# Lending another operand slot to plain products, and spreading row factors by two-part products, in a convolution and retention trunk

## The chip, the cores and the metric

The kernel runs on one core of one Trainium2 chip. The metric is device time in microseconds of one execution. A core has a matrix engine (TensorE, shown as PE, with its weight loads as PEld), three elementwise engines (VectorE as DVE, ScalarE as ACT, GpSimd as POOL) and SyncE (SP), from which this kernel issues its DMAs. Each engine works off its own queue strictly in the order in which the program was written out.

## The reference, cut to what matters

Sixteen meta rows are put ahead of 2048 rows of width 1024. Everything is float32.

```
hn   = rms_norm(h, norm1_g)
proj = hn @ w_in                            # 1024 x 4096, split into 8 parts
cx, cb, cc, cg, q, k, v, rg = split(proj, 8)
conv_out = cb * conv3(cc * cx) * silu(cg)
q, k = rotary(q, pos) * d**-0.5, rotary(k, pos)
ret  = group_norm(chunked_retention(q, k, v))   # 4 heads of 128, chunks of 128
out  = h + concat(conv_out, ret * silu(rg)) @ w_out
return rms_norm(out, final_g)[:, 16:]
```

The norm of a row is a factor per row, so the kernel multiplies the projected values by it instead of the inputs.

## The kernel before

The 2048 rows are handled as two blocks (r = 0 and 1) of 1024 rows, each as two halves (j) of 512. Per block there are four retention heads (`head`) and then four convolution groups (`conv_group`); each asks for two "quads", products of a 2 x 2 block matrix of weights (each block 4 tiles of 128 x 128 over the depth) with a 2 x 2 block matrix of rows. After both blocks follow eight output quads (`output`) with w_out as the moving side.

A quad is done in one of two ways. `quad` (line 208) forms seven products instead of eight: product number i multiplies a combination of weight blocks `w[i]` with a combination of row blocks `m[i]`. `quad_plain` (line 258) forms the eight plain products from the blocks `m[0]`, `m[7]`, `m[1]`, `m[5]` as they are. The first two quads of block 0, the first of block 1 and the first output quad are plain, since the combinations aren't ready by then. The combinations of the row side are called T1 (`m[3]`), T2 (`m[2]`), T3 (`m[4]`) and T4 (`m[6]`). `block_sums` makes them in the order T1, T2, T4, T3. For block 0 they are made on the spot; for block 1 and for w_out they are made earlier by `prepare`, put in DRAM (`sums_x`, `sums_w`) and fetched by `prepared(m, src, ns)`, where n = 0, 1, 2, 3 stands for T1, T2, T3, T4 (`SUMS`).

Each float32 operand is split into two float32r parts: hi, a rounding on ACT (line 99, or 102 with a scale), and lo, the rest on DVE (line 111, or 103). One product tile is three matmuls, lo by hi, hi by lo and hi by hi; a product of `quad` is 4 x 3 = 12 matmuls of 128 x 512, a plain quad is 96.

The parts of `m[i]` live in slots: one pair of tiles per i and depth tile kt, each a single buffer (`operand`). `m[7]` shares the slot of `m[4]` (`B12 = 4`). The weights of a plain quad also live in such slots: those of the first plain quad in slot 2 (`FIRST_W`), those of the others in slot 3 (`PLAIN_W`), the slot of T1. A slot can be rewritten once the last matmul that reads it is done. The raw weight tiles `ra` have 8 buffers.

The row factors: `row_factors` squares the rows on ACT (line 317), `spread_factors` makes the column of factors `rc`, and `spread` turns that column into a row that stands on all partitions (`rr`). It does so by a diagonal tile on DVE (line 281) and a float32 matmul with ones (line 288). The diagonal takes the tag `rot`, of which there is one buffer; `rotary` uses the same buffer for its products (lines 512 to 514 and the addition at line 108).

`spread` is called five times: for the meta rows (16 factors) and for j = 0, 1 of each block (512 factors).

The order of the work on each queue isn't written by hand: a planner runs the program through its own model of the costs ahead of time and, whenever an engine is free there, gives it the ready instruction that stands first in the program.

In block 0 the steps around the change, in the order of the program, are: splits of the row blocks, weights of both plain quads, `block_sums` with splits of T2 and T4, row factors, head 0 (plain quad, plain quad, `rest` with the splits of T1 and T3, attention), head 1 and so on.

Of the kernel before, what the change touches and what calls it, by code (L numbers as in the profile page):

```python
# [8 lines left out]
F32 = mybir.dt.float32  # L9
F32R = mybir.dt.float32r  # L10
BF16 = mybir.dt.bfloat16
AF = mybir.ActivationFunctionType
ALU = mybir.AluOpType

P = 128
# [6 lines left out]
HB = 512  # L22
NR = 2
BLK = SEQ // NR
CH = HB // P
KH = KT // 2
# [3 lines left out]
HIGH = 400  # L30
BRIEF = 2
BLOCK = ((0, 7), (1, 5))
FIRST_W, PLAIN_W, B12 = 2, 3, 4
SUMS = (3, 2, 4, 6)


# [32 lines left out]
def hybrid_trunk(ctx: ExitStack, tc: tile.TileContext, t, out: bass.AP, chunk_decay):  # L69
# [5 lines left out]
    nc = tc.nc  # L75
    x = t["x"]

    const = ctx.enter_context(tc.tile_pool(name="const", bufs=1))
    small = ctx.enter_context(tc.tile_pool(name="small", bufs=2))
    sb = ctx.enter_context(tc.tile_pool(name="sb", bufs=2))  # L80
# [15 lines left out]
    def split(hi, lo, src, scale=None, eng=nc.vector):  # L96

        if scale is None:
            nc.scalar.copy(out=hi, in_=src)  # L99
            sub(eng, lo, src, hi.bitcast(F32))  # L100
            return
        nc.scalar.mul(hi, src, scale)
        nc.vector.scalar_tensor_tensor(
            out=lo, in0=src, scalar=scale, in1=hi.bitcast(F32), op0=ALU.mult, op1=ALU.subtract
        )
# [39 lines left out]
    def parts(m, i, kt, src, factor=None):  # L145
        hi, lo = operand(i, kt)
        split(hi, lo, src, factor)
        m[i].append((hi, lo))
# [42 lines left out]
    def prepared(m, src, ns):  # L191

        for n in ns:
            for kt in range(KH):
                a = gen("t")[:, :HB]
                nc.sync.dma_start(a, src[n, kt])
                parts(m, SUMS[n], kt, a)
# [79 lines left out]
    def spread(col, n, dst, squares=None):  # L277

        a = col.shape[1]
        diag = sb.tile([P, HB], F32, name="rot", tag="rot", bufs=1).rearrange("p (a c) -> p a c", a=CH)  # L280
        nc.vector.tensor_tensor(
            out=diag[:n, :a, :n],
            in0=ident[:n, :n].rearrange("p (a c) -> p a c", a=1).broadcast_to([n, a, n]),
            in1=col.rearrange("p (a c) -> p a c", c=1).broadcast_to([n, a, n]),
            op=ALU.mult,
        )
        rp = ps_misc()
        nc.tensor.matmul(
            rp[:, : a * n].rearrange("p (a c) -> p a c", a=a), ones[:n].broadcast_to([n, P]), diag[:n, :a, :n], start=True, stop=True
        )  # L290
        nc.scalar.copy(out=dst, in_=rp[:, : a * n])
        if squares is not None:
            nc.scalar.activation(squares, rp[:, : a * n], AF.Square)

    gain = const.tile([P, KT], F32, name="gain")
    ident = const.tile([P, P], F32, name="ident")
    ones = const.tile([P, 1], F32, name="ones")
    neg_half = const.tile([P, CH], F32, name="neg_half")
    meta_s = const.tile([P, KT, NMETA], F32, name="meta_s")
# [344 lines left out]
    def output(pair, m, final_g):  # L644
        d = mixed[pair // 2]
        loads = [
            lambda a, i=i, k=k: nc.sync.dma_start(a.rearrange("p (k c) -> p k c", k=KH), d[pair % 2, i, k])
            for i in range(2)
            for k in range(2)
        ]  # L650
        ys = [[None, None], [None, None]]
        ss = small.tile([P, 2, 2], F32, name="so", tag="so")
        for i in range(2):
            for j in range(2):
                y = gen("yo")[:, :HB]
                row = (2 * pair + i) * P
                nc.sync.dma_start(y, x[row : row + P, j * HB : (j + 1) * HB])
                ys[i][j] = y
        last = [None]

        def take(i, j, pp, c):
            y = ys[i][j]
            if c is not None:
                add(nc.gpsimd, y, y, c)
            last[0] = nc.vector.tensor_tensor(out=y, in0=pp, in1=y, op=ALU.add)  # L665
            junk = sb.tile([P, HB], F32, name="rot", tag="rot", bufs=1)
            nc.scalar.activation(junk, y, AF.Square, accum_out=ss[:, i, j : j + 1])
            if i == j:
                ys[i][j] = gen("z")[:, :HB]
                nc.gpsimd.tensor_tensor(out=ys[i][j], in0=y, in1=final_g[:, j * HB : (j + 1) * HB], op=ALU.mult)  # L670

        if pair == 0:
            w = plain_parts(loads)
            prepared(m, sums_w, (1, 3))
            quad_plain(w, m, take)
            prepared(m, sums_w, (0, 2))
        else:
            quad(stationary(load_raw(loads)), m, take)
        for i in range(2):
            tot = small.tile([P, 1], F32, name="tot", tag="tot")  # L680
            add(nc.vector, tot, ss[:, i, 0:1], ss[:, i, 1:2])
            rs = small.tile([P, 1], F32, name="rf", tag="rf")
            rsqrt_mean(rs, tot)
            row = (2 * pair + i) * P
            for j in range(2):
                cs = slice(j * HB, (j + 1) * HB)
                y = ys[i][j]
                if i == j:
                    nc.scalar.mul(y, y, rs)
                else:  # L690
                    with tc.issue_after(last[0].ins):
                        nc.vector.scalar_tensor_tensor(
                            out=y, in0=y, scalar=rs, in1=final_g[:, cs], op0=ALU.mult, op1=ALU.mult
                        )
                nc.sync.dma_start(out[row : row + P, cs], y)

    make_identity(nc, ident)
    nc.gpsimd.memset(ones, 1.0)
    nc.gpsimd.memset(neg_half, -0.5)
    warm = const.tile([P, P], BF16, name="warm")  # L700
# [22 lines left out]
    for r in range(NR):  # L723
        f = factors[r]
        rot_t = sb.tile([P, 2, BLK], F32, name="rot_t", tag="rot_t", bufs=1)
        p0 = NMETA + r * BLK

        def load_tables():
            nc.sync.dma_start(rot_t, t["rot"][:, :, p0 : p0 + BLK])

        if r == 0:
            w = [None] * 4
            loads = w_loads(0)

            def begin(half):
                for n in (half, 2 + half):
                    w[n] = plain_part(n, loads[n], FIRST_W)

            m, b = moving(
                load_x(r), gain_of, {(0, 0): lambda: begin(0), (0, KH - 1): lambda: begin(1), (0, KT - 1): normalise_meta}  # L740
            )
            first = [[p for a, p in w]]
            blocks = None, meta_products([a for a, p in w])
            first.append(plain_parts(w_loads(1)))
            load_tables()
            nc.sync.dma_start(cols, t["cols"])
            t3 = [a[:, i * HB : (i + 1) * HB] for a in (row_tile("t3") for _ in range(2)) for i in range(2)]
            t1 = [brief("t1") if n < BRIEF else sb.tile([P, HB], F32, name="t1", tag="tc", bufs=COPIES) for n in range(KH)]
            for kt in range(KH):
                b11, b21, b12, b22 = (b[n * KH + kt] for n in range(4))  # L750
                block_sums(b11, b12, b22, b21, t1[kt], t3[kt], gain_of(kt), gain_of(KH + kt), nc.gpsimd)
                parts(m, 2, kt, b22)
                parts(m, 6, kt, b21)
            for _ in row_factors(0, f):
                pass
            nc.sync.dma_start(causal, t["causal"])
            nc.sync.dma_start(conv_w, t["conv_w"])
            nc.sync.dma_start(ret_g, t["ret_norm_g"])

            def rest():  # L760
                for i, held in ((3, t1), (4, t3)):
                    for kt in range(KH):
                        parts(m, i, kt, held[kt])

            between = (lambda: None, rest)
            later = prepare(load_x(1), sums_x, gain_of)
        else:
            m, b = moving(load_x(r), gain_of)
            first = [plain_parts(w_loads(0))]
            load_tables()  # L770
            prepared(m, sums_x, (1, 3))
            between = (lambda: prepared(m, sums_x, (0, 2)),)
            blocks = None, None
            later = prepare(load_w_out, sums_w)
        for h in range(NG):
            blocks = head(h, r, m, rot_t, f, blocks, lambda: ahead(r, h + 1), *((first, between) if h == 0 else ()))
            if h > 0:
                next(later, None)
                next(later, None)
        steps = row_factors(r + 1, factors[r + 1]) if r < NR - 1 else iter(())  # L780
        for g in range(NG):
            blocks = conv_group(g, r, m, f, blocks, lambda: ahead(r, NG + g + 1))
            for _ in range(3):
                next(steps, None)
# [44 lines left out]
```

## Time and profile before

| What | Value |
|---|---|
| Median of three runs | 902.29 us (902.17 to 903.6) |
| The profiled execution | 903.85 us, its span 902.1 us, 1.75 us around it |
| Mean granted TensorE clock | 0.994 |
| PE busy | 885.0 us (98%), 4407 matmuls |
| DVE busy | 714.6 us (79%) |
| ACT busy | 406.1 us (45%) |
| POOL busy | 398.9 us (44%) |
| Instructions | 12862 |

Matmuls are pipelined, so the busy time of PE overlaps itself: two matmuls of 128 x 512 start some 0.23 us apart while each lasts 0.39 us. Stalls are therefore read from the distance of starts, and from the waits. The profiled execution took 1.56 us more than the median.

### The profile page before, as it was taken

The page shows a single profiled execution, that of the slowest core. Times are in us where ns is not written, and L with a number is a line of the kernel's source. Part 1 is how long each engine was busy: PE and PEld are TensorE (multiplying, and loading weights), DVE is VectorE, ACT ScalarE, POOL GpSimd, SP SyncE. Part 2 cuts the span into 40 slices and gives each one's busy share as a digit, 9 for nine tenths or more (in the row PEclk, how much of TensorE's full clock was granted, in tenths as well). Part 3 has the DMA queues.
Part 4 walks back from the last instruction along what each step waited for, and adds up shares of the span by engine and source line. Part 5 has one row for each costly group of instructions (what it writes and reads, how often), then busy time and mean ns, then how long its engine had stood idle before and what let it go on. Part 6 is the DMA issues. An engine that isn't in the chain of part 4 may idle for free.

```text
span 902.1 us, 12862 instructions
## 1 busy us (share of the span) xinstructions
PE 885.0 (98%) x4407; PEld 727.8 (81%) x4407; DVE 714.6 (79%) x1173; ACT 406.1 (45%) x815; POOL 398.9 (44%) x294
## 2 busy tenths in 40 slices
PE   8998999999999999999999999999999999999996
PEld 5787888888878777788888888888888878788885
DVE  6798888897686776899889899777667697866764
ACT  8771342424344443655333332433333465554553
POOL 0533132323355554461333323345546445777763
PEclk9998999999999999999999999999999999999999
DMA  9711352623234232744125262113231685555532
GB/s 333 239 40 38 104 195 59 205 82 107 79 103 127 78 108 78 253 180 141 38 73 203 73 236 68 50 56 90 57 88 48 210 280 178 162 186 152 182 111 93
DMA packets 76242, 116.94 MB, mean 130 GB/s; under 512 B 7632, under 2 KB 24336, under 8 KB 76176
## 3 DMA queue, kind: packets, MB, share of 16 engines
q1 hardware_dynamic: 76176, 116.11, 40.1%
q8 instruction: 35, 0.57, 0.3%
q14 instruction: 31, 0.25, 0.1%
HBM read 90.92 MB, written 25.17 MB: 129 GB/s over the span
## 4 chain that ended last, share of the span: by engine, by line
PE 83%; DVE 9%; DMA 3%; ACT 2%; issue 2%; POOL 1%; SPq 0%; POOLq 0%; DVEq 0%; ACTq 0%
PE pj L208 66%; PE pj L258 7%; DVE ml L111 2%; DVE wl L111 2%; PE ms L611 2%; PE ms L612 1%; PE ms L601 1%; PE ms L588 1%; PE ms L392 1%; DVE rot L513 1%; DMA ra<-in_w_in 1%; PE ms L635 1%; PE ms L573 1%; DVE rot L512 1%; PE ms L578 1%
## 5 line engine op out<-in xcount | busy, mean ns | idle before, releaser
L208 PE MATMUL pj<-mh,wl 128*128 128x512 f32 x1008 | 400.0, 397 | 1.0 <-ACT tc L215 0.8
L208 PE MATMUL pj<-ml,wh 128*128 128x512 f32 x1008 | 394.2, 391 | 1.1 <-DVE ml L111 1.1
L208 PE MATMUL pj<-mh,wh 128*128 128x512 f32 x1008 | 393.4, 390 | 0.0
L99 ACT CAST wh<-ra 128x512 fp32r<-128x512 f32 x216 | 133.8, 620 | 315.1 <-PE pj L208 272.4
L208 PEld LDWEIGHTS pj<-mh,wl 128*128 128x128 f32 x1008 | 189.6, 188 | 43.1 <-ACT tc L215 2.2
L208 PEld LDWEIGHTS pj<-ml,wh 128*128 128x128 f32 x1008 | 189.8, 188 | 39.6 <-DVE ml L111 1.9
L208 PEld LDWEIGHTS pj<-mh,wh 128*128 128x128 f32 x1008 | 189.6, 188 | 39.8
L111 DVE TENSOR_TENSOR wl<-ra,wh 128x512 fp32r<-128x512 f32 x216 | 192.4, 892 | 36.2 <-ACT wh L99 35.2
L111 POOL TENSOR_TENSOR ra<-ra 128x512 f32<-128x512 f32 x72 | 113.0, 1570 | 82.0 <-DVE qg L556 32.3
L108 POOL TENSOR_TENSOR sa<-ra 128x512 f32<-128x512 f32 x36 | 54.9, 1525 | 122.6 <-DVE wl L111 62.1
L111 POOL TENSOR_TENSOR ra<-sa,ra 128x512 f32<-128x512 f32 x36 | 52.2, 1450 | 98.3 <-DVE wl L111 98.0
L215 ACT COPY tc<-pj 128x512 f32<-128x512 f32 x108 | 62.6, 580 | 0.0
L258 PE MATMUL pj<-ml,mh 128*128 128x512 f32 x128 | 50.8, 396 | 0.1
L258 PE MATMUL pj<-mh,mh 128*128 128x512 f32 x128 | 50.2, 395 | 0.0
L258 PE MATMUL pj<-mh,ml 128*128 128x512 f32 x128 | 48.5, 396 | 1.5 <-DVE ml L111 1.5
L624 POOL TENSOR_TENSOR rp<-rs,neg_half 128x4 f32<-128x4 f32 x16 | 19.9, 1245 | 51.0 <-DVE rs L108 50.8
L466 POOL TENSOR_TENSOR c<-c,rr 128x512 f32<-128x512 f32 x16 | 30.0, 1874 | 24.0 <-DVE c L454 13.6
L108 DVE TENSOR_TENSOR tc<-pj,tc 128x512 f32<-128x512 f32 x32 | 22.0, 688 | 23.4 <-PE pj L208 23.4
L111 DVE TENSOR_TENSOR ml<-t,mh 128x512 fp32r<-128x512 f32 x40 | 36.6, 961 | 0.8 <-ACT mh L99 0.8
L99 ACT CAST wh<-sa 128x512 fp32r<-128x512 f32 x36 | 22.3, 620 | 32.7 <-PE pj L208 32.7
L665 DVE TENSOR_TENSOR yo<-pj,yo 128x512 f32<-128x512 f32 x32 | 22.0, 688 | 18.8 <-POOL yo L108 8.9
L466 POOL TENSOR_TENSOR c<-c,tc 128x512 f32<-128x512 f32 x16 | 27.3, 1706 | 19.0 <-ACT tc L492 17.6
(128 smaller groups left out, 1134.3 us busy)
## 6 DMA issues: line engine op xcount, KB each, us to landing
ra<-in_w_in SPq DMA_DIRECT2D x128, 256.0 KB, 2.7
x<-in_xT SPq DMA_DIRECT2D x48, 256.0 KB, 5.1
w<-in_w_out SPq DMA_DIRECT2D x32, 256.0 KB, 5.0
ra<-mixed SPq DMA_DIRECT2D x32, 256.0 KB, 2.7
yo<-in_x SPq DMA_DIRECT2D x32, 256.0 KB, 4.4
ra<-in_x SPq DMA_DIRECT2D x16, 256.0 KB, 3.7
mixed<-qg SPq DMA_DIRECT2D x16, 256.0 KB, 2.3
sums_x<-x SPq DMA_DIRECT2D x16, 256.0 KB, 2.4
```

Source lines behind the costliest of these rows:

```text
L99: nc.scalar.copy(out=hi, in_=src)
L108: eng.tensor_tensor(out=out, in0=a, in1=b, op=ALU.add)
L111: eng.tensor_tensor(out=out, in0=a, in1=b, op=ALU.subtract)
L208: nc.tensor.matmul(bank, a[:, ks], b, start=first and kt == 0 and n == 0, stop=kt == KH - 1 and n == 2, skip_group_check=not first,)
L215: nc.scalar.copy(out=c, in_=bank)
L258: nc.tensor.matmul(banks[i], a[:, ks], b, start=half + kt + n == 0, stop=half == 1 and kt == KH - 1 and n == 2,)
L392: nc.tensor.matmul(four[i], meta_s[:, i % 2 * KH + kt, :], blocks[i][:, kt * P : (kt + 1) * P], start=kt == 0, stop=kt == KH - 1,)
L466: eng.tensor_tensor(out=out, in0=a, in1=b, op=ALU.mult)
L512: nc.vector.tensor_tensor(out=rot[:h, :w], in0=a[h:], in1=table[h:, 1, :], op=ALU.mult)
L611: nc.tensor.matmul(o[:, cs], pm[:, cs], vt[j][:, cs], start=True, stop=False)
L624: nc.gpsimd.tensor_tensor(out=rp, in0=rs, in1=neg_half.rearrange("p (c a) -> p c a", a=1), op=ALU.pow)
L665: last[0] = nc.vector.tensor_tensor(out=y, in0=pp, in1=y, op=ALU.add)
```

## The change

Three things change. Plain quads after the first put their weights in slot 6, T4's, instead of slot 3, T1's. Accordingly T1 is split where T4 was (together with T2), and T4 where T1 was (together with T3, and after it); the same exchange is made in the two places that fetch from DRAM. And `spread` no longer makes a diagonal: it splits the column of factors into hi and lo, and for each of up to four columns multiplies each part, broadcast over 128 columns as the stationary side, with a float32r unit matrix `ident_r`, so that two matmuls of 128 x 128 add up to the factors of 128 rows. `ident_r` is one more constant, copied once by ACT.

```diff
-FIRST_W, PLAIN_W, B12 = 2, 3, 4
+FIRST_W, PLAIN_W, B12 = 2, 6, 4
...
     def spread(col, n, dst, squares=None):
         a = col.shape[1]
-        diag = sb.tile([P, HB], F32, name="rot", tag="rot", bufs=1).rearrange("p (a c) -> p a c", a=CH)
-        nc.vector.tensor_tensor(
-            out=diag[:n, :a, :n],
-            in0=ident[:n, :n].rearrange("p (a c) -> p a c", a=1).broadcast_to([n, a, n]),
-            in1=col.rearrange("p (a c) -> p a c", c=1).broadcast_to([n, a, n]),
-            op=ALU.mult,
-        )
+        hi, lo = (small.tile([P, CH], F32R, name="ch", tag="ch", bufs=4) for _ in range(2))
+        split(hi[:n, :a], lo[:n, :a], col)
         rp = ps_misc()
-        nc.tensor.matmul(
-            rp[:, : a * n].rearrange("p (a c) -> p a c", a=a), ones[:n].broadcast_to([n, P]), diag[:n, :a, :n], start=True, stop=True
-        )
+        for c in range(a):
+            for p, part in enumerate((hi, lo)):
+                nc.tensor.matmul(
+                    rp[:, c * n : (c + 1) * n], part[:n, c : c + 1].broadcast_to([n, P]), ident_r[:n, :n],
+                    start=p == 0, stop=p == 1,
+                )
...
         if pair == 0:
             w = plain_parts(loads)
-            prepared(m, sums_w, (1, 3))
+            prepared(m, sums_w, (1, 0))
             quad_plain(w, m, take)
-            prepared(m, sums_w, (0, 2))
+            prepared(m, sums_w, (2, 3))
...
     make_identity(nc, ident)
+    nc.scalar.copy(out=ident_r, in_=ident)
...
                 parts(m, 2, kt, b22)
-                parts(m, 6, kt, b21)
+                parts(m, 3, kt, t1[kt])
...
             def rest():
-                for i, held in ((3, t1), (4, t3)):
+                for i, held in ((4, t3), (6, b[KH : 2 * KH])):
                     for kt in range(KH):
                         parts(m, i, kt, held[kt])
...
-            prepared(m, sums_x, (1, 3))
-            between = (lambda: prepared(m, sums_x, (0, 2)),)
+            prepared(m, sums_x, (1, 0))
+            between = (lambda: prepared(m, sums_x, (2, 3)),)
```

More of the change, by code (lines that the diff above doesn't have):

```diff
@@ L296, in hybrid_trunk @@
     ident = const.tile([P, P], F32, name="ident")
+    ident_r = const.tile([P, P], F32R, name="ident_r")
     ones = const.tile([P, 1], F32, name="ones")
```

## The prediction

> **What bounds the kernel now.** I read the page's busy shares, then the waits of PE, then the timeline around the longest.
>
> ```profile
> PE 885.0 (98%) x4407; PEld 727.8 (81%) x4407; DVE 714.6 (79%) x1173; ACT 406.1 (45%) x815; POOL 398.9 (44%) x294
> ```
> ```profile
> PE ms L611 <- DVE pm L603: 3.7, 1, 3.7
> ...
> PE pj L258 <- DVE ml L111: 1.5, 2, 1.2
> PE pj L208 <- DVE ml L111: 1.1, 2, 0.7
> PE pj L208 <- ACT tc L215: 0.8, 2, 0.7
> ```
>
> PE is the bound, so only work that PE sheds, or a place where it stands still, can pay. A wait's row gives the total, the number and the longest. The longest wait on PE's timeline, with the granted clock (the last figure but two of a window's row) and the chain's price for small float32 matmuls and for the two of `spread`:
>
> ```profile
> 75.45 0.39 PE L208 MATMUL pj<-ml,wh 128*128 128x512 f32 x1
> 75.67 0.39 PE L208 MATMUL pj<-mh,wh 128*128 128x512 f32 x1
> 79.81 0.79 PE L611 MATMUL ms<-kv,pm 128*128 128x128 f32 x2 [3.75 <-DVE pm L603]
> ...
> 83.24 0.77 PE L208 MATMUL pj<-mh,wl 128*128 128x512 f32 x1
> ...
> 85.52 0.42 PE L208 MATMUL pj<-mh,wh 128*128 128x512 f32 x1
> 85.77 0.40 PE L208 MATMUL pj<-mh,wl 128*128 128x512 f32 x1
> ```
> ```profile
> 79.50:83.00 3.50, 3.19 (x15) 3.19 (x16) 2.44 (x6) 0.00 (x0) 1.20 (x2) 0.50 0.19 75
> ```
> ```profile
> 121.26 0.89 PE ms L588 x8
> ...
> 297.83 1.05 PE ms L288 x2
> ```
>
> A large matmul takes 75.67 - 75.45 = 0.22 to 0.23 us of PE. So the stall in head 0 of block 0 is 79.81 - 75.67 - 0.23 = 3.91 us, and the clock is halved behind it. The 16 matmuls of lines 611 and 612 took 83.24 - 79.81 = 3.43 us; at 0.89 / 8 = 0.111 each they take 1.78, so 1.65 were lost. The five large ones from 83.24 to 85.52 took 2.28 instead of 1.14. Together the place costs 3.91 + 1.65 + 1.14 = 6.7 us. The Trainium skill ("TensorE: Matmul & The Clock Gate", Part 1, What's actually happening) says that about 3.4 us without work halve the clock and that it returns after about as long of steady work; the trace agrees, with 3.75 us idle and the usual pace back at 85.77. By that rule what is left of the stall would cost no more than its own length once it is under 3.4 us.
>
> Line 611 waits for pm, and pm for its turn on DVE:
>
> ```profile
> 28.00:43.00 15.00, 15.00 (x94) 12.13 (x93) 9.99 (x19) 12.28 (x36) 7.57 (x5) 1.00 0.81 266
> 43.00:54.00 11.00, 11.00 (x46) 8.38 (x46) 11.00 (x23) 10.07 (x23) 2.63 (x2) 1.00 0.37 128
> 54.00:79.00 25.00, 22.02 (x144) 18.07 (x142) 24.59 (x37) 12.10 (x29) 8.14 (x5) 0.99 0.12 32
> ```
> ```profile
> 35.38 0.16 DVE L108 TENSOR_TENSOR ss<-ss 128x4 f32<-128x4 f32 x1 [2.49 <-ACT ra L317]
> ...
> 49.68 0.68 DVE L281 TENSOR_TENSOR rot<-ident,rc 128x512 f32<-128x512 f32 x1
> ...
> 54.06 0.69 DVE L512 TENSOR_TENSOR rot<-kv,rot_t 64x512 f32<-64x512 f32 x1
> ...
> 58.23 1.68 DVE L513 TENSOR_TENSOR rot<-kv,rot_t 64x512 f32<-64x512 f32 x1
> 59.95 3.37 DVE L111 TENSOR_TENSOR ml<-t,mh 128x512 fp32r<-128x512 f32 x2
> ...
> 79.01 0.74 DVE L603 SCALAR_TENSOR_TENSOR pm<-ms,cols,causal 128x512 f32<-128x512 f32 x1
> ```
> ```profile
> 32.92 0.57 ACT L527 COPY kv<-pj 128x512 f32<-128x512 f32 x1
> ```
> ```profile
> 52.11 1.02 PE L288 MATMUL ms<-rot,ones 128*128 128x512 f32 x2
> ```
> ```profile
> 406.01 0.69 DVE L512 TENSOR_TENSOR rot<-kv,rot_t 64x512 f32<-64x512 f32 x1
> ```
>
> The third busy figure is DVE's: idle for 5.0 us of 28 to 43, then full to 79 (11.00 of 11, 24.59 of 25). Both halves of k and v are out of the first plain quad by 33.5 (the ACT copy), yet the first rotary step waits until 54.06, just behind the end of the second `spread` (53.13), whose diagonal holds the one `rot` buffer. In block 1, where no `spread` stands ahead of head 0, rotary runs at 406, while its plain quad still goes on, and PE shows no such stall there. That is what I expect here after the change.
>
> **The change, part by part.**
>
> *Rotary set free.* One rotary is four DVE steps of 0.69 us, 2.76; both of k are 5.5. Into the idle 5.0 us before 43 fit 5.0 of these. The diagonal at 49.68 goes too (0.68), for one small subtraction (0.15, below). So pm ends 5.0 + 0.5 = 5.5 us sooner, where 79.01 + 0.74 - 75.9 = 3.85 are needed: the stall goes, with 1.6 us to spare, and with it 6.7 us. If only one rotary fits, 2.76 + 0.5 = 3.3 come off, 0.6 of stall remains and the clock stays up. If none, 0.5. Bounds 0 to -6.7; I take -6.7, since block 1 is the nearest place and has the order wanted. Next late on DVE would be the group of lines 617 to 628 behind it, which the same 5.5 us relieve. Rows like 58.23 (1.68 us) and 59.95 (two in 3.37), where POOL is at work, show how DVE slips; that could eat the 1.6.
>
> *`spread` itself.* Prices:
>
> ```profile
> L327 DVE TENSOR_TENSOR rc<-rc 128x4 f32<-128x4 f32 x4 | 0.6, 152 | 0.0
> ...
> L291 ACT COPY rm<-ms 128x16 f32<-128x16 f32 x1 | 0.2, 172 | 1.3 <-PE ms L288 1.3
> ```
> ```profile
> 3.96 0.72 ACT L102 ACTIVATE mh<-x,gain 128x512 fp32r<-128x512 f32 x1 [1.73 <-DMA x<-in_xT]
> ```
>
> PE gives up 1.05 us a call (297.83) and takes on eight matmuls of 128 x 128 in float32r, a form the trace lacks. At the row of small float32 ones they take 0.89; at a quarter of a large float32r one (0.057) 0.46; if each logical one takes two such float32 passes, 1.78. Four calls of 512 factors: -0.6, between -2.4 and +2.9; I take the float32 row, the nearest in shape. (By the Trainium skill, same page, Back-to-back issue gap, a stream with 128 columns sustains about 81 ns each. That figure would give 8 x 0.081 = 0.65 a call and -1.6 in all. No run here shows it.) ACT takes on a small cast (0.17) and DVE a subtraction (0.15) on the way from `rc` to the matmuls. Both stand against the diagonal's 0.68. The call with 16 factors has two matmuls as before: nothing. The copy of `ident_r`, 128 x 128, lies in ACT's 1.73 us of idle time before 3.96; without that cover it would cost its own length, under the 0.72 of the row's larger tile.
>
> *T4 instead of T1.* The splits are equal in number and shape, as are the fetches. In block 0, T1 is ready before T4, so its splits can only come earlier, and the two brief buffers that hold it are free for kd and pm sooner. In `rest` T3 and T4 follow at the places of T1 and T3, where before each of their products came one (T3) or three (T4) products of 12 x 0.23 = 2.7 us sooner. Nothing in block 0 and 1; what hides it is this slack, and without it PE waits a split, 0.7 to 1.7 us. In the first seven-product output quad it pays:
>
> ```profile
> 765.42 3.24 DVE L111 TENSOR_TENSOR ml<-t,mh 128x512 fp32r<-128x512 f32 x3 [0.78 <-ACT mh L99]
> ...
> 769.18 4.66 DVE L111 TENSOR_TENSOR ml<-t,mh 128x512 fp32r<-128x512 f32 x4
> ```
>
> The last four splits are T3's, and product 4 waits for them: the 1.1 us in the list of waits. With T3 split first it is done by 768.7, and T4 by 773.8, ahead of product 6. -1.1, or 0 if the fetches come late (one is SP's queue, same count of DMAs).
>
> *Slot 6 is free later than slot 3.* The last product of a seven-product quad reads slot 6, product 3 reads slot 3. So the weights of the plain quads that open block 1 and the output can't be split before that last product. What PE does there now, and the splits of its last weights:
>
> ```profile
> 385.76 3.85 PE pj L258 x17
> 389.61 2.72 PE pj L208 x12
> ...
> 731.53 3.02 PE pj L258 x12
> 734.55 2.72 PE pj L208 x12
> 737.27 1.13 PE pj L258 x5
> 738.40 2.72 PE pj L208 x12
> ```
> ```profile
> L99 ACT CAST wh<-ra 128x512 fp32r<-128x512 f32 x216 | 133.8, 620 | 315.1 <-PE pj L208 272.4
> ```
> ```profile
> 384.03 0.68 DVE L111 TENSOR_TENSOR wl<-ra,wh 128x512 fp32r<-128x512 f32 x1
> ...
> 732.60 0.68 DVE L111 TENSOR_TENSOR wl<-ra,wh 128x512 fp32r<-128x512 f32 x1
> ```
>
> Plain matmuls (17 in both places, 3.85 and 4.15 us) run ahead of the last product, though its weights were there at 384.7 and 733.3. They must move behind it: no loss, as the product can move up. Two waits that these early weights cause go: 1.2 (L258 for ml) and 0.7 (L208 for tc, whose copy stands behind casts on ACT, some of them of those weights), -1.9. Against that the first plain weight is free when 3 of the last 12 matmuls are done, 2.05 us before the end, and needs a cast (0.62) and a subtraction (0.68): 1.4 with the handing over. It is hidden if both queues are clear, and 1.4 + 1.7 + 0.7 - 2.05 = 1.75 late if one long step (as at 58.23 on DVE, at 3.96 on ACT) stands ahead on each. I take half, 0.9 in each place: +1.8. Queued behind them are the later casts and splits of the row side, whose readers come 24 and more plain matmuls on. The raw weights keep their `ra` buffers about 6 us longer, which holds SP's next loads by as much. Those serve a quad that starts a whole plain quad, 96 x 0.23 = 22 us, later. POOL's queue gets nothing new. Sum here -0.1, between -1.9 and +1.6.
>
> **Sum.** -6.7 - 0.6 - 1.1 - 0.1 = -8.5: the span goes from 902.1 to 893.6, the profiled execution's 903.85 to 895.35. That execution stood 1.56 us over the median, so the median goes from 902.29 to 893.8.
>
> **The rivals.** *The stall moves.* The planner issues a matmul as soon as its own clock has the input ready, so DVE's slip may show at another place of head 0: 3 us of waits in all, at full clock. For it: the slow rows at 58.23 and 59.95. Against it: block 1. -3.7 - 1.8 = -5.5, 896.8.
>
> *It doesn't do what it says.* Rotary stays where it is for another reason, DVE saves 0.5 us, the half clock remains: -0.5, and half of the rest (-0.9): 900.9. For it: 2.49 us of that idle time is DVE standing behind an instruction already issued, which helps only if the planner saw it. Against it: the 0.9 us from 53.13 to 54.06.
>
> *Slower: slot 6 leaves PE empty.* If the last product stays at 389.6 and 738.4, nothing is left to run ahead of it. PE then idles 3.85 + 4.15 and the weights cost +1.8 behind it. With stalls of that length the clock is halved twice (2.8 each): +15.4, less 6.7 + 0.6 + 1.1, is +7.0, 909.3. It decides from some 4.2 us a place. Against it: the last weights' splits end at 384.7 and 733.3, before PE's plain matmuls end.
>
> **How the numbers follow.** Forecast 0.64, moved stall 0.17, nothing done 0.11, slot 6 0.06; 0.02 for the rest. The forecast's own range is 890.2 (-6.7 - 2.4 - 1.1 - 1.9) to 899.0 (+2.9 and +1.6 in place of -0.6 and -0.1). With the moved stall and the edge of the third case it is 890.0 to 900.6; 0.18 is left out. This measurement can tell about 0.2% (1.8 us) from no change. Faster: forecast, moved stall and a part of the third, 0.84; same 0.10; slower 0.06.
>
> **What would show it.** Right: rotary of k before 50 us; no wait of line 611 over 1 us before 90; clock 1.00 from 20 us on; no plain matmul ahead of the last product near 385 and 735; product 4 of the first seven-product output quad without a wait. Wrong: a gap of PE of 2 us or more before the first plain matmul of block 1 or of the output, or rotary still behind 53 us.

## The result, and the profile after

The change made the kernel slower: 909.92 us against 902.29 (medians of six runs each), a ratio of 1.0081 with an interval of 1.0068 to 1.0094. The forecast was 893.8 us, in a range of 890.0 to 900.6.

The profiled execution after took 908.13 us (span 906.4, mean clock 0.997). The five others took 909.74 to 910.27 at a clock of 0.993, 1.8 us longer in the median; a likely reason is given at the output, below. The engines, from the page, and PE's waits:

```profile
PE 884.7 (98%) x4431; PEld 728.0 (80%) x4431; DVE 708.8 (78%) x1173; ACT 408.8 (45%) x821; POOL 397.3 (44%) x294
```
```profile
PE pj L258 <- DVE ml L111: 6.7, 2, 3.8
...
PE pj L208 <- ACT tc L215: 2.0, 2, 1.2
PE pj L208 <- DVE wl L111: 1.6, 2, 1.2
PE ms L285 <- DVE ch L111: 1.0, 1, 1.0
```

The wait of 3.7 us for `pm` is gone. At the head of the list stands a wait that was 1.5 us before: plain quads for the low parts of their weights, 6.7 us in two places.

Where the time went shows when each kernel reaches the same large matmul (128x512, lines 208 and 258, in the order of their starts in the trace):

| n-th large matmul | what lies there | before, us | after, us | difference |
|---|---|---|---|---|
| 192 | block 0, head 0 | 55.73 | 55.31 | -0.4 |
| 240 | before the old `pm` stall | 72.94 | 75.77 | +2.8 |
| 300 | behind the old stall | 96.47 | 92.57 | -3.9 |
| 1300 | late in block 0 | 371.51 | 367.56 | -4.0 |
| 1390 | in block 1's plain quad | 393.08 | 395.21 | +2.1 |
| 2700 | late in block 1 | 729.97 | 732.04 | +2.1 |
| 2800 | in the plain output quad | 754.10 | 758.47 | +4.4 |
| 3408 | the last | 894.56 | 898.91 | +4.4 |

So block 0 gives 4.0 us, the start of block 1 takes 6.1, the start of the output 2.3, and nothing else moves.

**Block 0.** DVE's windows (third busy figure), then its rows and PE's:

```profile
28.00:43.00 15.00, 15.00 (x98) 11.95 (x97) 12.10 (x23) 10.64 (x33) 3.81 (x3) 1.00 0.76 241
43.00:54.00 11.00, 11.00 (x50) 9.11 (x49) 10.99 (x19) 9.38 (x21) 8.28 (x4) 1.00 0.51 185
54.00:79.00 25.00, 22.83 (x152) 18.71 (x151) 24.12 (x41) 13.20 (x33) 8.91 (x6) 1.00 0.11 32
```
```profile
27.52 1.67 DVE L511 TENSOR_TENSOR rot<-kv,rot_t 64x512 f32<-64x512 f32 x1
29.21 1.70 DVE L512 TENSOR_TENSOR rot<-kv,rot_t 64x512 f32<-64x512 f32 x1
...
56.86 0.69 DVE L111 TENSOR_TENSOR ml<-x,mh 128x512 fp32r<-128x512 f32 x1
57.47 0.16 DVE L111 TENSOR_TENSOR ch<-rc,ch 128x4 fp32r<-128x4 f32 x1
...
76.86 0.74 DVE L602 SCALAR_TENSOR_TENSOR pm<-ms,cols,causal 128x512 f32<-128x512 f32 x1
```
```profile
57.68 1.00 PE L285 MATMUL ms<-ident_r,ch 128*128 128x128 f32 x7 [0.99 <-DVE ch L111]
...
68.68 0.47 PE L208 MATMUL pj<-mh,wl 128*128 128x512 f32 x1 [1.17 <-DVE wl L111]
...
78.73 0.38 PE L610 MATMUL ms<-kv,pm 128*128 128x128 f32 x2
```

Rotary of k starts at 27.5 us instead of 54, as forecast, and PE no longer waits for `pm`. But DVE took up 2.1 us of its idle time before 43 us (12.10 busy instead of 9.99), not 5.0; two of the first rotary steps take 1.7 us instead of 0.69; and it is still full to 79 us (24.12 of 25). `pm` ends at 77.60 instead of 79.75, 2.15 us sooner and not 5.5. The table shows what came of it: from the 240th to the 300th matmul PE needs 16.80 us instead of 23.53, the whole 6.7 of the forecast. But between the 192nd and the 240th it loses 3.2. Of these, 2.2 are the two new waits on DVE: for the small subtraction of `spread`, behind a split, and for a weight's low part. Another 0.9 are seven matmuls of the second `spread` (57.68 to 58.60), whose work stood ahead of the 192nd before.

Those losses are part of the reason why the stall is gone. PE was ready for `pm` at 75.90 before and is ready for it at 78.73 now, behind the same 252 large matmuls: 2.83 us later. `pm` came 2.15 us sooner, and 3.85 were needed. With PE as early as before, some 1.7 us of the stall (77.60 - 75.90) would have been left; that is an estimate.

**The start of block 1.** Before, the low parts of the first plain weights stood ahead of the last row splits in DVE's queue:

```profile
382.22 1.89 DVE L111 TENSOR_TENSOR ml<-ra,mh 128x512 fp32r<-128x512 f32 x3
...
385.23 2.51 DVE L103 SCALAR_TENSOR_TENSOR ml<-x,gain,mh 128x512 fp32r<-128x512 f32 x3
```

ACT, DVE and PE after, then PE's stretches (first busy figure, and the clock, the last but two):

```profile
383.39 0.62 ACT L99 CAST mh<-ra 128x512 fp32r<-128x512 f32 x1
```
```profile
383.82 0.68 DVE L465 TENSOR_TENSOR c<-tc,c 128x512 f32<-128x512 f32 x1
384.43 0.75 DVE L103 SCALAR_TENSOR_TENSOR ml<-x,gain,mh 128x512 fp32r<-128x512 f32 x1
385.09 0.68 DVE L108 TENSOR_TENSOR tc<-pj,tc 128x512 f32<-128x512 f32 x1
385.69 1.82 DVE L103 SCALAR_TENSOR_TENSOR ml<-x,gain,mh 128x512 fp32r<-128x512 f32 x2
387.44 0.68 DVE L111 TENSOR_TENSOR ml<-t,mh 128x512 fp32r<-128x512 f32 x1
388.04 0.68 DVE L111 TENSOR_TENSOR ml<-ra,mh 128x512 fp32r<-128x512 f32 x1
```
```profile
384.60 0.39 PE L208 MATMUL pj<-mh,wh 128*128 128x512 f32 x1
388.77 0.79 PE L258 MATMUL pj<-mh,ml 128*128 128x512 f32 x1 [3.79 <-DVE ml L111]
389.36 0.63 PE L258 MATMUL pj<-ml,mh 128*128 128x512 f32 x1
```
```profile
384.00:388.70 4.70, 0.98 (x5) 0.48 (x3) 4.70 (x8) 4.70 (x11) 1.72 (x1) 1.00 0.60 222
388.70:392.20 3.50, 3.43 (x8) 2.75 (x9) 3.50 (x4) 1.55 (x3) 2.89 (x2) 0.51 0.25 75
392.20:396.00 3.80, 3.80 (x18) 3.13 (x18) 3.80 (x6) 0.63 (x1) 1.61 (x1) 1.00 0.41 120
```

The high part of the first plain weight (`mh<-ra`) is ready at 384.01. Its low part (`ml<-ra`) is formed on DVE from 388.04, behind a convolution step, a row split (`ml<-x`), another convolution step, two more row splits and a split of a combination: 4.0 us, 2.4 of them row splits. PE ends its last product at 384.6 + 0.23 and stands 3.94 us. Then the clock is 0.51 for 3.5 us; eight steps take 3.48 us instead of 1.81, another 1.7.

**The start of the output.** The windows around the same wait, here 2.88 us, in this profile and in that of the experiment weights_ahead, which has the same stall:

```profile
738.00:741.30 3.30, 0.42 (x3) 0.01 (x1) 3.30 (x6) 3.09 (x6) 1.49 (x1) 1.00 1.02 387
741.30:745.00 3.70, 3.70 (x16) 3.05 (x17) 3.70 (x7) 1.92 (x4) 1.15 (x1) 1.00 0.70 224
```
```profile
741.00:744.00 3.00, 3.00 (x9) 2.35 (x8) 3.00 (x5) 1.90 (x4) 1.13 (x1) 0.53 0.58 150
```

In the profile after, the clock stays up behind the stall; in that of weights_ahead it is 0.53, and from the 2700th to the 2800th large matmul PE needs 28.0 us instead of 26.43. Those 1.6 us are about what separates the profiled execution from the five others, whose mean clock is lower. That they lose it at this place is inferred, as only one execution has a trace.

### The profile page after: what moved, and what is told of

The parts are those of the page before. It is cut to its first block, busy times and chain, and to the rows that moved or that the text cites. A ratio compares the mean times of both kernels' runs of the same rounds, so it can differ in the third digit from the quotient of the medians.

```text
span 906.4 us, 12916 instructions
## 1 busy us (share of the span) xinstructions
PE 884.7 (98%) x4431; PEld 728.0 (80%) x4431; DVE 708.8 (78%) x1173; ACT 408.8 (45%) x821; POOL 397.3 (44%) x294
## 4 chain that ended last, share of the span: by engine, by line
PE 82%; DVE 9%; DMA 4%; ACT 2%; issue 2%; POOL 1%; SPq 0%; POOLq 0%; ACTq 0%; DVEq 0%
PE pj L208 66%; PE pj L258 7%; DVE ml L111 2%; DVE wl L111 1%; PE ms L610 1%; PE ms L611 1%; PE ms L600 1%; PE ms L587 1%; DMA x<-in_xT 1%; DMA t<-sums_x 1%; PE ms L391 1%; PE ms L634 1%; PE ms L572 1%; DMA ra<-in_x 1%; PE ms L577 1%
## 5 line engine op out<-in xcount | busy, mean ns | idle before, releaser
L258 PEld LDWEIGHTS pj<-mh,ml 128*128 128x128 f32 x128 | 24.3, 191 | 14.4 <-DVE ml L111 8.4
```

What stands on the lines that cost most here:

```text
L258: nc.tensor.matmul(banks[i], a[:, ks], b, start=half + kt + n == 0, stop=half == 1 and kt == KH - 1 and n == 2,)
```

## The experiments

For block 0 two theories stood against each other: the gain comes from the freed `rot` buffer alone (A), or from the exchange of T1 and T4 (B). For the starts of block 1 and of the output: slot 6 is free too late (C, the prediction's slower rival is near it), or the low parts of the plain weights stand in DVE's queue behind the row splits (A1). In the later kernels a few line numbers differ by up to three.

**spread_only**: the kernel before with the new `spread` alone.

```diff
-        diag = sb.tile([P, HB], F32, name="rot", tag="rot", bufs=1)...
+        hi, lo = (small.tile([P, CH], F32R, name="ch", tag="ch", bufs=4) for _ in range(2))
```

> The kernel before with the new spread alone: the slots, the fetches and the order of T1 and T4 stay as before. Theory A (the gain of block 0 comes from the rot buffer that the diagonal no longer holds): rotary of k starts before 36 us, no wait of PE for pm over 1 us, position of the 300th large matmul about 4 us sooner than before (92 to 93 us instead of 96.5), median 897 to 899. Theory B (the gain comes from T1 being split early, which frees its brief buffers): the wait for pm stays, median 901.5 to 902.5. Both: no plain-weight stall at block 1 or the output.

905.28 us, ratio 1.0027 (1.0016 to 1.0039): slower than before. Its waits, and windows around the second of them:

```profile
PE pj L208 <- DVE wl L111: 3.2, 2, 2.6
...
PE ms L610 <- DVE pm L602: 1.9, 1, 1.9
```
```profile
130.50:133.00 2.50, 0.66 (x3) 0.20 (x2) 2.33 (x7) 0.62 (x1) 0.00 (x0) 1.00 0.32 105
133.00:136.00 3.00, 2.97 (x17) 2.97 (x18) 2.04 (x5) 0.00 (x0) 1.17 (x2) 0.68 0.30 87
136.00:140.00 4.00, 4.00 (x16) 3.15 (x16) 2.83 (x14) 0.51 (x1) 1.41 (x2) 0.81 0.01 4
```

The old stall is gone here too (the 300th large matmul at 93.76), but waits of 2.6 us for a weight (at 67.86) and of 1.9 us for `pm` of head 1 (at 133.03) take its place, the second with a lowered clock behind it. From the 400th to the 800th large matmul it needs 123.81 us, the kernel before 120.24. Rotary of k starts at 27.5 here as after. A falls as far as it promised the gain.

**slots_only**: the kernel before with the slots and T1/T4 exchanged, and the old `spread`.

```diff
-FIRST_W, PLAIN_W, B12 = 2, 3, 4
+FIRST_W, PLAIN_W, B12 = 2, 6, 4
```

> The kernel before with slot 6 for the weights and the exchange of T1 and T4, the old spread with its diagonal. Theory A: the stall for pm near 76 us stays or shrinks little, and the two stalls before the first plain matmul of block 1 and of the output are there (4 us with half clock, 3 us): 902.3 + 6.1 + 2.3 to 4.1 = 910.7 to 912.5. Theory B: the stall for pm is gone, as in the changed kernel, 909 to 910.

915.56 us, ratio 1.0140 (1.0120 to 1.0159). It has both stalls for plain weights (6.7 us in the list, as after), and in block 0 the pattern of spread_only: the 300th matmul early, at 91.30, then waits up to the 800th at 247.69 (before 246.52). B falls with A: the old stall is gone with either half, and only both together keep the time.

With one half alone it is not an earlier `pm` that removes the stall. There `pm` comes later than before, and PE's order has one or two more products of 12 large matmuls ahead of its use:

| Kernel | `pm` of head 0 ends, us | PE starts its matmul, us | large matmuls ahead of it |
|---|---|---|---|
| before | 79.75 | 79.81 | 252 |
| after | 77.60 | 78.73 | 252 |
| spread_only | 81.79 | 84.02 | 264 |
| own_diag (next) | 82.60 | 84.84 | 264 |
| slots_only | 82.63 | 84.28 | 276 |

In slots_only rotary of k starts only at 55.73, behind the diagonal, as before. Why the planner chose these orders is not shown.

**own_diag**: the kernel before, with a buffer of its own for the diagonal (room from padding of the brief tiles).

```diff
-        diag = sb.tile([P, HB], F32, name="rot", tag="rot", bufs=1)...
+        diag = sb.tile([P, HB], F32, name="dg", tag="dg", bufs=1)...
```

> The kernel before, only that the diagonal of spread has a buffer of its own instead of the one of rotary (the padding of the brief buffers is taken away to make room). If it is the buffer that moves rotary forward, this behaves in block 0 as the new spread alone did: rotary of k before 40 us, no wait over 1 us for pm near 76 us, the 300th large matmul at 93 to 94.5 us, median within 2 us of 905.3. If the two-part products themselves did it, it stays as before: rotary at 54 us, 901.5 to 903.5.

905.92 us, ratio 1.0036 (1.0024 to 1.0049), with the pattern of spread_only. Its waits:

```profile
PE pj L208 <- DVE wl L111: 5.0, 2, 4.3
...
PE ms L611 <- DVE pm L603: 2.0, 1, 2.0
```

Rotary of k starts at 27.78. So it is the shared buffer that held rotary back, and not the price of the diagonal; and freeing it alone does not pay.

**block0_only**: the new `spread` and the exchange in block 0; slot 3 and the old order of the fetches in block 1 and at the output.

```diff
-FIRST_W, PLAIN_W, B12 = 2, 6, 4
+FIRST_W, PLAIN_W, B12 = 2, 3, 4
...
-            first.append(plain_parts(w_loads(1)))
+            first.append(plain_parts(w_loads(1), 6))
...
-            prepared(m, sums_x, (1, 0))
-            between = (lambda: prepared(m, sums_x, (2, 3)),)
+            prepared(m, sums_x, (1, 3))
+            between = (lambda: prepared(m, sums_x, (0, 2)),)
```

> The changed kernel with slot 6 and the exchange of T1 and T4 kept in block 0 alone, where slot 6 is free from the start; block 1 and the output use slot 3 and the old order of fetches. Theory A: the gain of block 0 without the two losses, 897.5 to 899.5, and within 1 us of the new spread alone. Theory B: the same median, but 3 us or more faster than the new spread alone. If block 1 or the output lose time here too, the loss isn't slot 6's: over 901.

898.77 us, ratio 0.9964 (0.9949 to 0.9979): faster than both kernels. The 300th large matmul starts at 92.49 and the 1300th at 367.45, as after; the last at 891.65, 7.3 us sooner. The whole loss of the change lies in block 1 and the output.

**weights_ahead**: the changed kernel with the weights of those plain quads written ahead of the second half of the row splits in the program.

```diff
-            m, b = moving(load_x(r), gain_of)
-            first = [plain_parts(w_loads(0))]
+            first = []
+            m, b = moving(load_x(r), gain_of, {(0, KT - 1): lambda: first.append(plain_parts(w_loads(0)))})
```

> The changed kernel, with the weights of the plain quads of block 1 and of the output put ahead of the second half of the row splits in the program, all else equal. Theory A (the weights are split late because their lo parts stand behind row splits on DVE): the stall before the first plain matmul shrinks from 3.95 us with half clock and 3.0 us to under 1.5 us each, 900 to 904. Theory C (slot 6's release itself bounds, whatever the queue): waits of 2.5 us or more stay in both places, 907 to 910.

909.45 us, ratio 1.0077 (1.0061 to 1.0094): no change. DVE's order came out the same and the two stalls kept their lengths (6.7 us in the list). The planner picks among the instructions that are ready; that the row splits were ready while the weight's slot was still taken fits this, but is inferred. This run decides nothing between A1 and C.

**weights_first**: as weights_ahead, and the low parts of the second half of the row splits are put behind the plain weights' low parts in DVE's queue, by a constraint.

```diff
-            for half in range(2):
+            with hold() if j else nullcontext():     # hold: issue after the last low part of the plain weights
...
```

> The changed kernel with slot 6 throughout; on DVE alone, the lo parts of the second half of the row blocks (8 of 16) are queued behind the lo parts of the plain weights, in block 1 and in the output. Theory A1 (the weights wait for DVE, which works through row splits that nobody needs yet): the wait before the first plain matmul of block 1 falls from 3.8 us to under 1.5 us without half clock behind it, that of the output from 2.9 to under 1.5: 902 to 905. Theory C (the release of slot 6 bounds): both waits stay above 2.5 us, 908 to 910.

899.76 us, ratio 0.9966 (0.9953 to 0.9978). DVE and PE at the start of block 1, and PE's waits:

```profile
383.48 0.68 DVE L110 TENSOR_TENSOR ml<-ra,mh 128x512 fp32r<-128x512 f32 x1
...
391.44 0.74 DVE L102 SCALAR_TENSOR_TENSOR ml<-x,gain,mh 128x512 fp32r<-128x512 f32 x1
```
```profile
384.21 0.50 PE L260 MATMUL pj<-mh,ml 128*128 128x512 f32 x1 [0.85 <-DVE ml L110]
```
```profile
PE pj L260 <- DVE ml L110: 1.3, 2, 0.9
```

With slot 6 kept and only the queue's order changed, 6.7 us of wait become 1.3 and the time falls by 10.2 us against the changed kernel. That is A1; what C can claim is 1.3 us.

**slot3_late**: the reverse, from block0_only. Slot 3 is free early, but the plain weights' low parts are queued behind all 16 row splits.

```diff
-            first = [plain_parts(w_loads(0))]
+            with tc.issue_after(row_made[-1].ins):
+                first = [plain_parts(w_loads(0))]
```

> The kernel with the change in block 0 alone (slot 3 in block 1 and the output, 898.8 us), but with the lo parts of the plain weights queued on DVE behind all 16 row splits. The slot is free as early as before. Theory A1: losing the early place on DVE is enough to bring the stall back: a wait of 2 us or more before the first plain matmul of block 1, 902 to 907. Theory C: slot 3 keeps its early release, the stall stays away, 898 to 900.

913.17 us, ratio 1.0114 (1.0101 to 1.0128). PE at the same place, and its waits:

```profile
390.03 0.80 PE L261 MATMUL pj<-mh,ml 128*128 128x512 f32 x1 [5.94 <-DVE ml L110]
```
```profile
PE pj L261 <- DVE ml L110: 10.0, 3, 5.9
```

The high parts of the plain weights are cast on ACT from 375.10, and their low parts are formed on DVE only from 389.30. The stall is there without slot 6. Queue order alone makes it, and C falls.

**slot2**: block0_only, with these plain weights in slot 2 (T2's), and T1 and T4 fetched first.

```diff
-FIRST_W, PLAIN_W, B12 = 2, 3, 4
+FIRST_W, PLAIN_W, B12 = 2, 2, 4
```

> The kernel with the change in block 0 alone, and in block 1 and the output the weights in slot 2 (T2's, read by product 2, freed earlier than slot 3), T1 and T4 fetched first, T2 and T3 later. Theories A1 and C: the first plain matmul of block 1 and of the output comes no later than with slot 3, no wait over 1.3 us there; T2 is now the late one, needed by product 2, so a wait of 0 to 3 us may come at product 2 of the first quad behind the plain one: 897.5 to 902.

899.31 us, ratio 0.9963 (0.9949 to 0.9977), not to be told from block0_only. Its first plain matmuls of block 1 start at 374.68, 10 us before PE runs out of other work in the profile after (384.8), and the longest wait of a plain quad for a low part is 0.5 us.

**first_t4_last**: weights_first, with T4's splits in block 0 written behind head 0's attention.

```diff
-                for i, held in ((4, t3), (6, b[KH : 2 * KH])):
+            def last():
+                for kt in range(KH):
+                    parts(m, 6, kt, b[KH + kt])
```

> The changed kernel with the low parts of the second half's row splits queued behind those of the plain weights (in block 1 and at the output), as in weights_first, and besides this the splits of T4's weights in block 0 traced after head 0's attention instead of together with T3's. If the waits of 1.26 us at 56 us and 1.35 us at 67 us in block 0 come from VectorE having T4's low parts ahead of attention's work, they shrink and the time is 896.5 to 898.8. If VectorE is late there for the row work itself, they stay and the time is that of weights_first, 899.0 to 900.4. Over 901 would say that T4's weights, now split later, are themselves waited for.

899.67 us, ratio 0.9961 (0.9947 to 0.9974), as weights_first. The wait for `ch` shrinks from 1.0 to 0.4 us, that for `wl` stays at 1.17. T4's splits explain at most the first. In its profile the waits of plain quads for low parts are longer (3.0 us against 1.3); most of that lies ahead of 20 us, and why is not shown.

**first_slot3**: weights_first's order on DVE with slot 3 and the old fetches.

```diff
-FIRST_W, PLAIN_W, B12 = 2, 6, 4
+FIRST_W, PLAIN_W, B12 = 2, 3, 4
```

> Block 0 as in the changed kernel; in block 1 and at the output the weights of the plain products go through slot 3 again with the fetch order of before, but VectorE's order is that of weights_first: the low parts of the second half's row splits behind the plain weights' low parts. If only VectorE's queue sets how long TensorE waits there, the slot makes no difference and the time is that of weights_first, 899 to 900.5, or that of block0_only, 898 to 899. If slot 6 being free earlier buys something once the queue is right, this one is slower than weights_first by what it buys, 1 to 2 us (901 to 902).

900.90 us, ratio 0.9976 (0.9965 to 0.9986). It falls between the two expected times and its interval overlaps that of weights_first (0.9953 to 0.9978), so it does not decide. The waits of its plain quads for low parts are no shorter in sum: one of 1.2 us at the output (727.22), against 0.9 and 0.4 us in block 1 with slot 6. If the exchange is worth anything once the order is right, it is about 1 us. Of the versions faster than both kernels, block0_only, slot2, weights_first and first_t4_last can't be told apart.

## Why the prediction was wrong

**The step that failed is the term for slot 6** ("1.75 late if one long step ... stands ahead on each", "I take half, 0.9 in each place"), together with "Queued behind them are the later casts and splits of the row side". It was the other way round: on DVE the row splits and convolution steps stood ahead of the weights' low parts, 4.0 us of them, and no single long step. The upper bound of that term was +1.6 for both places; measured were +6.1 and +2.3, in most runs probably some 1.6 more by the clock. The prediction had named a gap of 2 us or more at these places as a sign of being wrong; the gaps are 3.79 and 2.88 us. A weight that is ready late goes behind all that the planner could issue before. The bound would have had to count the work ready on DVE at that moment: in the trace before, DVE shows no idle time from 378 to 391 us.

**The rival with 0.06 (slot 6 leaves PE empty, 909.3)** has the right place, the right sign and nearly the time of 909.92, but not its cause. It let the last product stay late and PE idle for the plain matmuls that used to run ahead. The product did move up (it ends at 384.8), as the forecast said. PE then waited for DVE's queue. That its time came so near is luck.

**Rotary set free**: the first half of the mechanism held. Rotary started at 27.5, but `pm` ended 2.15 us sooner and not 5.5, which alone would not have covered the 3.85 needed. The old stall with its half clock went all the same, since PE came to `pm` 2.83 us later. The -6.7 for the place is mis-sized, at -3.9: 3.2 us were lost just ahead, 2.2 of them in two new waits on a DVE that stayed full. The forecast had 1.6 us to spare "that could eat" the slip; the slip was larger, and the rival "the stall moves" (-3.7) describes block 0 better. spread_only shows that it could have moved much worse.

**The exchange in block 0, costed at nothing**, is worth something there: spread_only and block0_only differ by it and by the slot of block 0's second plain quad, 905.28 against 898.77. Why there are waits of 2.6 us at 68 and of 1.9 us at 133 us without it is not settled; the runs show only their places and that DVE is late there.

**`spread`**: the price of its matmuls was about right. Seven of its matmuls and the step to the next work, in the profile after:

```profile
338.21 0.99 PE L285 MATMUL ms<-ident_r,ch 128*128 128x128 f32 x7
339.04 0.45 PE L208 MATMUL pj<-mh,wl 128*128 128x512 f32 x1
```

That is 0.83 / 7 = 0.12 each, near the row of 0.111 taken, so 0.95 a call against 1.05. The way to them was not free: the small subtraction, put against the diagonal's 0.68, is what PE waits 0.99 us for at 57.68. The Trainium skill's 81 ns for a stream with 128 columns ("TensorE: Matmul & The Clock Gate", Part 2, Back-to-back issue gap) does not hold for this form here.

**The first seven-product output quad (-1.1)** gave nothing: from the 2800th large matmul to the last it is 140.46 us before and 140.44 after. The wait for `ml` is gone, and another stands in its place; ACT's rows and PE's:

```profile
774.31 0.62 ACT L99 CAST wh<-ra 128x512 fp32r<-128x512 f32 x1 [0.40 <-PE pj L208]
774.83 1.07 ACT L215 COPY tc<-pj 128x512 f32<-128x512 f32 x2
```
```profile
775.47 0.50 PE L208 MATMUL pj<-mh,wl 128*128 128x512 f32 x1 [1.19 <-ACT tc L215]
...
778.94 0.47 PE L208 MATMUL pj<-mh,wl 128*128 128x512 f32 x1 [0.46 <-DVE wl L111]
```

PE now waits for a copy on ACT that stands behind a weight's cast, and then for a low part on DVE.

**The sum** came out, in the profiled spans, as -4.0 + 6.1 + 2.3 = +4.4, and 906.4 - 902.1 = +4.3. The medians differ by 7.6, since the profiled execution stood 1.56 us above its median before, and 1.79 below it after.

## What to carry to other kernels

When an operand becomes ready later, ask what its engine's queue holds by then: in an order made by readiness, it goes behind everything that is ready, even if the matmul engine needs it first. Writing it earlier in the program changed nothing here, a constraint on the order 10.2 us. A stall removed in a stretch where an engine stays full is only worth its length less the waits that the same engine makes elsewhere, so each part of a change is to be tried alone and together.

## What the runs showed of the hardware that was not expected

In these traces the clock did not follow a fixed length of idle time. Behind 1.87 us of waiting in spread_only its mean was 0.68 and 0.81 in the two stretches shown. PE's steps there had their usual length for another 1.0 us, up to 134.03. Then they were about twice as long up to 137.40 (0.43 us instead of 0.23 for a large matmul). Behind 2.88 us in the profile after the clock stayed at 1.00, and behind the same 2.88 us in weights_ahead it was 0.53. The prediction took from the Trainium skill ("TensorE: Matmul & The Clock Gate", Part 1, What's actually happening) that about 3.4 us without work halve the clock, and concluded that a shorter stall costs only its own length; these rows differ, and the measurement decides. Nor was the pace back after 3.4 us of work behind the old stall: the prediction's own rows show long steps from 79.81 to 85.52. On top of its own length a stall of 1.9 us or more cost between nothing (741.30) and 2.8 us (79.81 before, 1.65 + 1.14); at 388.77 it was 1.7.

Two rotary steps of the same shape took 1.67 and 1.70 us at 27.52 and 29.21, where the one at 54.06 in the profile before took 0.69. GpSimd was busy for 2.20 of the 2.20 us from 27.0 and for 1.16 of the 1.80 from 29.2. From 35.27, where it was idle, the same two steps took 0.69 each. No run here shows that it is the cause. The prediction's 2.76 us for one rotary is a price for a quiet time; the profile before already had these rows, whose means (1183 and 872 ns) are well above 0.69:

```profile
L513 DVE TENSOR_TENSOR rot<-kv,rot_t 64x512 f32<-64x512 f32 x16 | 18.9, 1183 | 0.2
...
L512 DVE TENSOR_TENSOR rot<-kv,rot_t 64x512 f32<-64x512 f32 x16 | 14.0, 872 | 1.9 <-ACT kv L527 1.4
```
